# Low parts of 23 weight chunks by an accumulating transfer, one Strassen unit less and a reordered final norm in a residual decoder block

## The chip, the cores and the metric

One core of a Trainium2 chip runs the whole block. Its engines are TensorE (PE; PEld is its weight load), VectorE (DVE), ScalarE (ACT) and GpSimd (POOL); SyncE (SP) issues transfers. The metric is the device time of one execution in microseconds, the median of several runs. The time before is 1468.63 us (three runs, 1467.74 to 1469.05).

## The reference

For 16 learned meta tokens and 256 tokens of 2048 features, in float32:

```python
hn = rms_norm(h, norm_mix_g)
u, gb_in, gc_in, v_in, ga_lin, gbr_lin = split(hn @ w_in)          # 2048 x 12288
y_a = einsum(causal_multiscale_pool(u), pool_w) * pool_scale
y_b = (gb_in * causal_depthwise_conv(gc_in * v_in, conv_w)) @ conv_out_w
h = h + (sigmoid(ga_lin + b) * y_a + sigmoid(gbr_lin + b) * y_b) @ w_o
hn = rms_norm(h, norm_ffn_g)
gate, up = split(hn @ w_gate_up)                                   # 2048 x 11264
h = h + (silu(gate) * up) @ w_down                                 # 5632 x 2048
out = rms_norm(h, norm_final_g)[:, N_META:]
```

## The kernel before

**Split products.** Every float32 weight is split into a high part (the value rounded to the engine's fp32r type) and a low part (the value minus the high part); activations likewise. A product is three matmuls into one accumulation: high by high, high by low, low by high (`mm3`, L500; the second, L503, is the one that reads the weights' low part).

**The weight stream.** All weights come as 528 chunks of 128 partitions x 1024 columns (512 KB), in the order of use. `load` (L109) puts a chunk into one of five raw buffers, by a transfer that SP issues. `split_weights` (L132) makes the high part by a pass of ScalarE (`cut`, L129) and the low part by a subtraction of VectorE that needs the raw chunk and the high part (L130). The parts go into a ring of pairs of tiles, three at first, six from the output projection on (`homes`). `advance` (L164) is called when TensorE takes a job: it gives back the tiles of jobs before that one, issues loads up to five chunks ahead of what is split, and splits as many further jobs as the ring has room for.

**Stages.** After the input projection, pooling, convolution and gates, come 19 groups: two of the output projection, then three rounds of gate/up groups (4, 4 and 3) followed by two down groups each. A group (`group`, L506) has four PSUM banks for its four output blocks ("11", "12", "21", "22": row block and column block of a 256 x 1024 result) and walks a plan of pairs of chunks. A plain pair takes its two chunks one after the other; each gives three matmuls of 512 columns in each of the four banks, 12 in all. A Strassen unit takes a pair as one job of four pairs of tiles, with 7 products of three matmuls, and VectorE builds the sums of blocks for it (L149 to L153). `plan_of` (L714) and `groups` (L720) say at which places units stand. `job_list` (L735) makes the list of jobs from the plans: a plain chunk is a job of kind 1, a unit one of kind 4.

**The end.** In the last down group the last `HELD` = 2 pairs are kept back (`kept`): TensorE first does all others for all banks, then the four kept chunks bank by bank, in the order 11, 12, 21, 22, so that the final norm of a block can start while the next bank is worked on. The last bank is done in two halves of 256 columns. `finish` (L639) takes a finished piece: square with row sums on ScalarE, product with the norm's weights on VectorE, the running sum of squares, and with a row block's last piece the reciprocal root (`rsqrt`, L315), four scalings and the output transfers. Row block 0 ends with bank 12, row block 1 with the second half of 22.

**Order.** Instructions are put into each engine's list when the kernel is built, by priority and by the readiness that is expected then; on the chip each list runs in order, and waits hold it.

Of the kernel before, what the change touches and what calls it, by code (L numbers as in the profile page):

```python
# [10 lines left out]
AF = mybir.ActivationFunctionType  # L11
ALU = mybir.AluOpType
PSUM = bass.MemoryType.PSUM

P = 128
D = 2048
# [21 lines left out]
BC = BW * P  # L38
NC = D // BC
NB = SEQ // P  # L40
FC = FF // BC
# [12 lines left out]
def block_kernel(ctx: ExitStack, tc: tile.TileContext, xT, xn, gfin, consts, spread, weights, out):  # L54
# [6 lines left out]
    nc = tc.nc  # L61
# [44 lines left out]
    raws = {}  # L106
    n_chunks = weights.shape[0]
# [22 lines left out]
        nc.vector.tensor_tensor(out=lo, in0=raw, in1=hi, op=ALU.subtract)  # L130

    def split_weights(j, parts=1):  # L132
        kind, c = jobs[j]
        if kind == 1:
            raw = raws.pop(c)
            hi, lo = part(j)
            step = CH * P // parts
            for s in range(0, CH * P, step):
                q = slice(s, s + step)
                cut(hi[:, q], lo[:, q], raw[:, q])  # L140
            splits[j] = hi, lo
        else:

            r0, r1_ = raws.pop(c), raws.pop(c + 1)
            b12, b11, b22, b21 = r0[:, :BC], r0[:, BC:], r1_[:, :BC], r1_[:, BC:]
            ta = sums.tile([P, 2 * BC], F32, name="ta")
            td = sums.tile([P, 2 * BC], F32, name="td")
            (ah, al), (bh, bl), (ch, cl), (dh, dl) = [part(j) for _ in range(4)]
            nc.vector.tensor_tensor(out=ta[:, :BC], in0=b11, in1=b12, op=ALU.add)  # L149
            cut(bh[:, :BC], bl[:, :BC], b11)  # L150
            nc.vector.tensor_tensor(out=ta[:, BC:], in0=b12, in1=b22, op=ALU.add)
            nc.vector.tensor_tensor(out=td[:, :BC], in0=ta[:, :BC], in1=b22, op=ALU.add)
            nc.vector.tensor_tensor(out=td[:, BC:], in0=td[:, :BC], in1=b21, op=ALU.add)  # L153
            cut(ah, al, ta)
            cut(dh, dl, td)
            cut(ch, cl, r1_)
            splits[j] = {"b11": (bh[:, :BC], bl[:, :BC]),
                         "t1": (ah[:, :BC], al[:, :BC]), "t3": (ah[:, BC:], al[:, BC:]),
                         "t2": (dh[:, :BC], dl[:, :BC]), "t4": (dh[:, BC:], dl[:, BC:]),
                         "b22": (ch[:, :BC], cl[:, :BC]), "b21": (ch[:, BC:], cl[:, BC:])}  # L160
        state["ready"] = j + 1
        state["cut"] = c + (1 if kind == 1 else 2)
# [451 lines left out]
    c = 0  # L614
    tail = {}
    for ci, n in enumerate(CHUNKS):
        af = {"order": iter(["a"] * slots["a"])}
        for i in range(n):
            late = {}
            if c == 0:  # L620
                late[KT // 2 - 4] = lambda: turn_h(NC - 2, "q")
                late[KT // 2 - 2] = lambda: turn_h(NC - 1, "q")
            elif i > 0:
                late[KT // 2 - 3] = lambda c=c, i=i: turn_a(c - 1, af, 2 * (i - 1))
            gate_up(c, late)
            c += 1
        last = ci == len(CHUNKS) - 1
        if last:
            after.close()
            fin = scope.enter_context(tc.tile_pool(name="fin", bufs=1))  # L630
            gf = fin.tile([P, D], F32, name="gf")
            nc.gpsimd.dma_start(out=gf, in_=gfin)
            hg = fin.tile([P, NB, D], F32, name="hg")
            junk = fin.tile([P, BC], F32, name="junk")
            sq = fin.tile([P, NB, NC + 1], F32, name="sq")
            st = fin.tile([P, NB, 7], F32, name="st")
            preload = fin.tile([P, 1], F32, name="preload")

        def finish(b, i, q):  # L639

            h = hn[:, b, q]
            nc.scalar.activation(out=junk[:, : q.stop - q.start], in_=h, func=AF.Square, accum_out=sq[:, b, i : i + 1])
            nc.vector.tensor_tensor(out=hg[:, b, q], in0=h, in1=gf[:, q], op=ALU.mult)
            base, ms, sd, y, y2, m2, r = [st[:, b, i : i + 1] for i in range(7)]
            part_ = sq[:, b, i : i + 1]
            if i == 0:
                nc.scalar.activation(out=preload, in_=ones[:, 0:1], func=AF.Sqrt)
            elif i == 1:
                binary(base, sq[:, b, 0:1], part_, ALU.add)
                mean(base, base)  # L650
            elif i < NC:
                nc.vector.scalar_tensor_tensor(out=base, in0=part_, scalar=1.0 / D, in1=base, op0=ALU.mult, op1=ALU.add)
            else:
                nc.vector.scalar_tensor_tensor(out=ms, in0=part_, scalar=1.0 / D, in1=base, op0=ALU.mult, op1=ALU.add)
                rsqrt(r, ms, sd, y, y2, m2)
                for n_ in (0, 2, 1, 3):
                    o = hg[:, b, n_ * BC : (n_ + 1) * BC]
                    if n_ == 2:
                        nc.scalar.activation(out=o, in_=o, func=AF.Copy, scale=r)
                    else:  # L660
                        nc.vector.tensor_scalar(out=o, in0=o, scalar1=r, scalar2=None, op0=ALU.mult)
                    (nc.sync if n_ < 2 else nc.scalar).dma_start(
                        out=out[b * P : (b + 1) * P, n_ * BC : (n_ + 1) * BC], in_=o)

        for g in range(NC // 2):
            late = {2 * n - 2: lambda: turn_a(c - 1, af, 2 * (n - 1))} if g == 0 else {}
            ends = last and g == NC // 2 - 1
            plain, e, kept, step = group(af, late, HELD if ends else 0)
            keys = [f"{b + 1}{i + 1}" for b in range(NB) for i in range(2)]
            for key in keys:  # L670
                b, cb = int(key[0]) - 1, 2 * g + int(key[1]) - 1
                h = hn[:, b, cb * BC : (cb + 1) * BC]
                binary(h, h, e[key], ALU.add)
            for key in keys:
                b, cb = int(key[0]) - 1, 2 * g + int(key[1]) - 1
                h = hn[:, b, cb * BC : (cb + 1) * BC]
                if ends and key == "22":
                    binary(h, plain[key], h, ALU.add)
                    for i in range(2):
                        q = slice(i * BC // 2, (i + 1) * BC // 2)  # L680
                        p = bank("q")[:, : BC // 2]
                        for n_, (f, k, w) in enumerate(kept):
                            mm3(p, f[f"a2{k + 1}"], [x[:, BC + q.start : BC + q.stop] for x in w], n_ == 0,
                                n_ == len(kept) - 1)
                        binary(h[:, q], p, h[:, q], ALU.add)
                        finish(b, cb + i, slice(cb * BC + q.start, cb * BC + q.stop))
                    continue
                for f, k, w in kept:
                    step(f, k, w, (key,))
                binary(h, plain[key], h, ALU.add)  # L690
                if last:
                    finish(b, NC if cb == NC - 1 else cb, slice(cb * BC, (cb + 1) * BC))
    scope.close()


HELD = 2
STRASSEN = 3
CHUNKS = (4, 4, 3)
FORMS = ("a11", "a12", "a22", "s1", "s2", "s3", "s4", "a21")
# [14 lines left out]
def plan_of(n, at):  # L714

    marked, plain = iter(range(len(at))), iter(range(len(at), n))
    return [(next(marked), True) if i in at else (next(plain), False) for i in range(n)]


def groups():  # L720


    for g in range(NC // 2):
        yield "out", 0, g, plan_of(KT // 2, ((2, 5), (0, 3))[g])
    c = 0
    for n in CHUNKS:
        for i in range(n):
            at = (0, 3) if c + i == 0 else (1, 4) if (n - i) % 2 else (0, 3, 6)
            yield "up", c + i, 0, plan_of(KT // 2, at)
        for g in range(NC // 2):  # L730
            yield "down", c, g, plan_of(2 * n, (0, 3))
        c += n


def job_list(n_chunks):  # L735

    tail = [s for *_, plan in groups() for _, s in plan]
    c = n_chunks - 2 * len(tail)
    jobs = [(1, i) for i in range(c)]
    for s in tail:  # L740
        jobs += [(4, c)] if s else [(1, c), (1, c + 1)]
        c += 2
    return jobs

# [67 lines left out]
```

## Time and profile before

| what | value |
|---|---|
| median of three runs | 1468.63 us (1467.74 to 1469.05) |
| profiled execution | 1469.13 us |
| its span, first to last instruction | 1467.3 us |
| TensorE busy | 1452.2 us, 7682 matmuls |
| VectorE busy | 1137.0 us |
| ScalarE busy | 746.5 us |
| GpSimd busy | 4.9 us |
| mean granted TensorE clock | 0.998 |
| bytes read from HBM | 285.38 MB, 196 GB/s over the span |

A row of the timeline is: start, duration, engine, line, operation, output<-inputs, shape, count, and in brackets the idle time before it with what ended it. Neighbouring rows of the same kind are merged into one with a count. A line can be that of a helper: L243 is `binary`, L129 and L130 are `cut`, L253 and L254 are `split` with a scale.

### The profile page before, as it was taken

How to read it: one execution, taken by the hardware profiler on the slowest of the kernel's cores; microseconds unless marked ns; L12 is line 12 of the kernel's file. 1: busy time of each engine (PE TensorE's matmuls, PEld its weight loads, DVE VectorE, ACT ScalarE, POOL GpSimd, SP SyncE). 2: the span in 40 equal slices, each digit the busy share in tenths (PEclk: the TensorE clock that was granted, in tenths of full speed). 3: DMA queues.
4: the chain of work that ended last, by engine and by line, in shares of the span. 5: the costliest groups of instructions: out<-in, count | busy, mean ns of one | idle time of the engine just before them, and what ended most of it. 6: DMA issues, size and time to landing. Idle time of an engine off the chain costs nothing.

```text
span 1467.3 us, 20054 instructions
## 1 busy us (share of the span) xinstructions
PE 1452.2 (99%) x7682; PEld 1251.5 (85%) x7682; DVE 1137.0 (77%) x1510; ACT 746.5 (51%) x925; POOL 4.9 (0%) x12
## 2 busy tenths in 40 slices
PE   9999999999999999999999999999999999999997
PEld 9999999999888888888888888888888888887886
DVE  7986666666656565658998989988898998788898
ACT  6544444444444444445675556554555555455563
POOL 0000000000000000000000000000000000000000
PEclk9999999999999999999999999999999999999999
DMA  9555555555665656666655557655555765564663
GB/s 334 192 185 186 186 187 187 187 186 182 207 217 190 218 186 214 190 192 217 216 169 190 172 199 219 211 175 197 191 196 188 229 201 185 189 200 159 216 215 115
DMA packets 79984, 288.80 MB, mean 197 GB/s; under 512 B 8976, under 2 KB 9232, under 8 KB 79632
## 3 DMA queue, kind: packets, MB, share of 16 engines
q1 hardware_dynamic: 77760, 279.61, 58.3%
q0 software_dynamic: 1120, 6.29, 1.3%
q10 hardware_dynamic: 1008, 1.61, 0.3%
q8 instruction: 60, 0.98, 0.3%
q14 instruction: 36, 0.29, 0.1%
HBM read 285.38 MB, written 2.10 MB: 196 GB/s over the span
## 4 chain that ended last, share of the span: by engine, by line
PE 96%; DVE 2%; DMA 1%; ACT 0%; issue 0%; ACTq 0%; DVEq 0%
PE acc L504 17%; PE acc L502 17%; PE acc L503 17%; PE acc L200 6%; PE acc L199 6%; PE acc L198 6%; PE acc L219 6%; PE acc L220 6%; PE acc L221 6%; PE acc L213 4%; PE acc L214 2%; PE acc L277 1%; DVE lo L130 1%; DMA raw<-weights 1%; DVE act L243 0%; PE acc L367 0%
## 5 line engine op out<-in xcount | busy, mean ns | idle before, releaser
L130 DVE TENSOR_TENSOR lo<-raw,hi 128x1024 fp32r<-128x1024 f32 (+1 forms) x529 | 618.3, 1177 | 241.9 <-ACT hi L129 238.9
L129 ACT CAST hi<-raw 128x1024 fp32r<-128x1024 f32 (+1 forms) x529 | 533.0, 1016 | 528.2 <-PE acc L504 154.5
L502 PE MATMUL acc<-hi,hp 128*128 128x512 f32 x678 | 263.3, 391 | 2.5 <-ACT hp L253 1.0
L503 PE MATMUL acc<-lo,hp 128*128 128x512 f32 x678 | 263.6, 389 | 0.0
L504 PE MATMUL acc<-hi,hp 128*128 128x512 f32 x678 | 263.6, 390 | 0.0
L219 PE MATMUL acc<-xp,hi 128*128 128x258 f32 (+3 forms) x704 | 198.7, 282 | 0.0
L220 PE MATMUL acc<-xp,hi 128*128 128x258 f32 (+3 forms) x704 | 198.5, 282 | 0.0
L221 PE MATMUL acc<-xp,lo 128*128 128x258 f32 (+3 forms) x704 | 198.4, 282 | 0.0
L503 PE MATMUL acc<-lo,act 128*128 128x512 f32 (+1 forms) x468 | 181.3, 387 | 0.0
L502 PE MATMUL acc<-hi,act 128*128 128x512 f32 (+1 forms) x468 | 180.7, 388 | 0.3 <-DVE act L243 0.3
L504 PE MATMUL acc<-hi,act 128*128 128x512 f32 (+1 forms) x468 | 180.2, 388 | 0.3 <-DVE act L251 0.3
L502 PEld LDWEIGHTS acc<-hi,hp 128*128 128x128 f32 x678 | 127.0, 188 | 30.8 <-ACT hi L129 2.5
L503 PEld LDWEIGHTS acc<-lo,hp 128*128 128x128 f32 x678 | 127.3, 188 | 26.4
L504 PEld LDWEIGHTS acc<-hi,hp 128*128 128x128 f32 x678 | 127.3, 188 | 26.3
L219 PEld LDWEIGHTS acc<-xp,hi 128*128 128x128 f32 x704 | 132.4, 188 | 0.7
L221 PEld LDWEIGHTS acc<-xp,lo 128*128 128x128 f32 x704 | 132.5, 188 | 0.0
L220 PEld LDWEIGHTS acc<-xp,hi 128*128 128x128 f32 x704 | 132.4, 188 | 0.0
L502 PEld LDWEIGHTS acc<-hi,act 128*128 128x128 f32 x468 | 87.8, 188 | 18.8 <-ACT act L250 0.8
L504 PEld LDWEIGHTS acc<-hi,act 128*128 128x128 f32 x468 | 87.7, 188 | 18.9 <-DVE act L251 1.2
L503 PEld LDWEIGHTS acc<-lo,act 128*128 128x128 f32 x468 | 87.9, 188 | 17.9
L198 PE MATMUL acc<-hi,xp 128*128 128x512 f32 x256 | 100.0, 390 | 0.0
L200 PE MATMUL acc<-hi,xp 128*128 128x512 f32 x256 | 99.6, 389 | 0.0
(133 smaller groups left out, 1747.0 us busy)
## 6 DMA issues: line engine op xcount, KB each, us to landing
raw<-weights SPq DMA_DIRECT2D x527, 512.0 KB, 3.8
sp<-spread POOLq DMA_DIRECT2D x4, 768.0 KB, 5.9
hn<-xn POOLq DMA_DIRECT2D x1, 2048.0 KB, 11.9
xall<-xT SPq DMA_DIRECT2D x7, 272.0 KB, 7.2
gf<-gfin POOLq DMA_DIRECT2D x1, 1024.0 KB, 6.8
out<-hg ACTq DMA_DIRECT2D x4, 256.0 KB, 3.4
out<-hg SPq DMA_DIRECT2D x4, 256.0 KB, 3.1
raw<-weights ACTq DMA_DIRECT2D x2, 256.0 KB, 4.9
```

The lines of the kernel that those rows point to most:

```text
L129: nc.scalar.copy(out=hi, in_=raw)
L130: nc.vector.tensor_tensor(out=lo, in0=raw, in1=hi, op=ALU.subtract)
L198: nc.tensor.matmul(out=p, lhsT=a[:, 0, t], rhs=hi, start=first, stop=False)
L199: nc.tensor.matmul(out=p, lhsT=a[:, 0, t], rhs=lo, start=False, stop=False)
L200: nc.tensor.matmul(out=p, lhsT=a[:, 1, t], rhs=hi, start=False, stop=last)
L213: nc.tensor.matmul(out=p, lhsT=hi, rhs=a[:, :, off : off + SEQ], start=first, stop=False)
L219: nc.tensor.matmul(out=p, lhsT=hi, rhs=a[:, 0, off : off + n], start=first, stop=False)
L220: nc.tensor.matmul(out=p, lhsT=hi, rhs=a[:, 1, off : off + n], start=False, stop=False)
L221: nc.tensor.matmul(out=p, lhsT=lo, rhs=a[:, 0, off : off + n], start=False, stop=last)
L502: nc.tensor.matmul(out=p, lhsT=ah, rhs=wh, start=first, stop=False)
L503: nc.tensor.matmul(out=p, lhsT=ah, rhs=wl, start=False, stop=False)
L504: nc.tensor.matmul(out=p, lhsT=al, rhs=wh, start=False, stop=last)
```

## The change

In the job list each job gets a third entry, `added`. It is true for a plain chunk of the output projection or later, if the job before it isn't one and the last five jobs are all plain; with the kernel's plans that holds for 23 chunks. For these `split_weights` makes the high part as before, then ScalarE writes the negated high part into the low tile, and GpSimd issues a transfer of the same chunk from HBM with an addition into that tile: low = -high + weight. VectorE's subtraction isn't issued.

In the last group of the last round the plan has one Strassen unit (at place 0) instead of two (at 0 and 3), and `HELD` is 3: six plain chunks are kept. They are the last six jobs, and the second, fourth and sixth of them are added ones.

`finish` is cut into `square`, `weigh`, `gather` and `finish`. For the last bank both halves are done first (matmuls, addition, square), then the first half is weighed, both sums are gathered, and the second half is weighed between them and the reciprocal root.

```diff
+            raw = raws.pop(c)
+            hi, lo = part(j)
+            nc.scalar.copy(out=hi, in_=raw)
+            nc.scalar.activation(out=lo, in_=hi, func=AF.Copy, scale=-1.0)
+            nc.gpsimd.dma_start(out=lo, in_=weights[c], accum_op=ALU.add)
+            splits[j] = hi, lo
...
-        def finish(b, i, q):
...
+        def square(b, i, q):
+            nc.scalar.activation(out=junk[:, : q.stop - q.start], in_=hn[:, b, q], func=AF.Square,
+                                 accum_out=sq[:, b, i : i + 1])
...
+        def weigh(b, q):
+            nc.vector.tensor_tensor(out=hg[:, b, q], in0=hn[:, b, q], in1=gf[:, q], op=ALU.mult)
+        def gather(b, i):
...
+        def finish(b, between=lambda: None):
+            ms, sd, y, y2, m2, r = [st[:, b, i : i + 1] for i in range(1, 7)]
+            between()
+            rsqrt(r, ms, sd, y, y2, m2)
...
-                        finish(b, cb + i, slice(cb * BC + q.start, cb * BC + q.stop))
+                        square(b, cb + i, where[i])
+                    weigh(b, where[0])
+                    gather(b, cb)
+                    gather(b, cb + 1)
+                    finish(b, lambda: weigh(b, where[1]))
...
-HELD = 2
+HELD = 3
...
-            yield "down", c, g, plan_of(2 * n, (0, 3))
+            yield "down", c, g, plan_of(2 * n, (0,) if c + n == FC and g == 1 else (0, 3))
...
-        jobs += [(4, c)] if s else [(1, c), (1, c + 1)]
+        for k in range(1 if s else 2):
+            added = not s and len(jobs) > n_chunks - 2 * len(tail) + 5 and not jobs[-1][2] \
+                and all(j[0] == 1 for j in jobs[-5:])
+            jobs.append((4 if s else 1, c + k, added))
```

## Rows read from the trace of the kernel before

**Rows 1.** The page: busy us by engine, and the chain that ended last.
```profile
PE 1452.2 (99%) x7682; PEld 1251.5 (85%) x7682; DVE 1137.0 (77%) x1510; ACT 746.5 (51%) x925; POOL 4.9 (0%) x12
...
PE 96%; DVE 2%; DMA 1%; ACT 0%; issue 0%; ACTq 0%; DVEq 0%
```
**Rows 2.** Waits of TensorE: waiting line, waited for, us in total, times, longest.
```profile
PE acc L502 <- ACT hp L253: 1.0, 1, 1.0
PE acc L502 <- ACT hi L129: 1.0, 2, 0.5
PE acc L502 <- DVE act L243: 0.8, 2, 0.5
```
**Rows 3.** Windows, the last group: length, busy us by engine, clock, DMA share, GB/s.
```profile
1425.70:1457.40 31.70, 31.61 (x151) 26.48 (x149) 30.97 (x54) 16.24 (x29) 0.00 (x0) 1.00 0.24 84
```
**Rows 4.** Timeline of TensorE, kept steps: eight matmuls apart, then 23 halves apart.
```profile
1446.12 0.39 PE L502 MATMUL acc<-hi,act 128*128 128x512 f32 x1
...
1447.93 0.39 PE L504 MATMUL acc<-hi,act 128*128 128x512 f32 x1
...
1454.28 0.28 PE L502 MATMUL acc<-hi,act 128*128 128x256 f32 x1
...
1457.03 0.28 PE L504 MATMUL acc<-hi,act 128*128 128x256 f32 x1
```
**Rows 5.** Groups by form: busy us, mean ns, idle before and what ended it.
```profile
L130 DVE TENSOR_TENSOR lo<-raw,hi 128x1024 fp32r<-128x1024 f32 x485 | 588.7, 1222 | 239.7 <-ACT hi L129 236.9
L129 ACT CAST hi<-raw 128x1024 fp32r<-128x1024 f32 x485 | 506.2, 1052 | 494.7 <-PE acc L200 145.7 <-PE acc L504 123.1 <-PE acc L220 108.4
```
**Rows 6.** DMA issues of the page: KB each, median us from issue to landing.
```profile
raw<-weights SPq DMA_DIRECT2D x527, 512.0 KB, 3.8
sp<-spread POOLq DMA_DIRECT2D x4, 768.0 KB, 5.9
hn<-xn POOLq DMA_DIRECT2D x1, 2048.0 KB, 11.9
...
gf<-gfin POOLq DMA_DIRECT2D x1, 1024.0 KB, 6.8
```
**Rows 7.** Timeline, one chunk: ScalarE's high part, TensorE's first use of the low part.
```profile
985.12 1.05 ACT L129 CAST hi<-raw 128x1024 fp32r<-128x1024 f32 x1
...
998.47 0.39 PE L503 MATMUL acc<-lo,act 128*128 128x512 f32 x1
```
**Rows 8.** Timeline of ScalarE and TensorE at the start of unit m = 4, first gate/up group.
```profile
768.21 1.05 ACT L129 CAST hi<-raw 128x1024 fp32r<-128x1024 f32 x1 [0.48 <-PE acc L277]
769.16 0.47 ACT L253 ACTIVATE hp<-acc,cst 128x256 fp32r<-128x256 f32 x1
...
769.68 0.50 PE L502 MATMUL acc<-hi,hp 128*128 128x512 f32 x1 [1.05 <-ACT hp L253]
```
**Rows 9.** Timeline of TensorE, end of the first kept bank, with two L502 merged.
```profile
1448.16 0.62 PE L502 MATMUL acc<-hi,act 128*128 128x512 f32 x2
1448.61 0.39 PE L503 MATMUL acc<-lo,act 128*128 128x512 f32 x1
```
**Rows 10.** Timeline of ScalarE and VectorE, a unit's addition in front of a split.
```profile
778.22 1.05 ACT L129 CAST hi<-raw 128x1024 fp32r<-128x1024 f32 x1 [1.30 <-issue]
...
780.32 0.69 DVE L151 TENSOR_TENSOR ta<-raw 128x512 f32<-128x512 f32 x1 [1.51 <-DMA raw<-weights]
780.92 1.22 DVE L130 TENSOR_TENSOR lo<-raw,hi 128x1024 fp32r<-128x1024 f32 x1
```
**Rows 11.** Timeline behind the last matmul.
```profile
1457.35 0.42 DVE L243 TENSOR_TENSOR hn<-acc,hn 128x256 f32<-128x256 f32 x1 [0.31 <-PE acc L504]
...
1457.69 1.27 DVE L661 TENSOR_SCALAR hg<-hg,st 128x512 f32<-128x512 f32 x3
...
1459.80 0.20 ACT L316 ACTIVATE st<-st 128x1 f32<-128x1 f32 x1 [1.21 <-DVE st L654]
...
1460.82 1.28 DVE L661 TENSOR_SCALAR hg<-hg,st 128x512 f32<-128x512 f32 x3
```

More of the change, by code (lines that the diff above doesn't have):

```diff
@@ L132, in split_weights @@
     def split_weights(j, parts=1):
-        kind, c = jobs[j]
-        if kind == 1:
+        kind, c, added = jobs[j]
+        if added:
+            raw = raws.pop(c)
[4 more added lines that the diff above has]
+            splits[j] = hi, lo
+        elif kind == 1:
             raw = raws.pop(c)
@@ L637, in block_kernel @@
             preload = fin.tile([P, 1], F32, name="preload")
-        def finish(b, i, q):
[L641 to L645, printed above, removed]
+        def square(b, i, q):
+            nc.scalar.activation(out=junk[:, : q.stop - q.start], in_=hn[:, b, q], func=AF.Square,
+                                 accum_out=sq[:, b, i : i + 1])
@@ L646, in finish @@
             if i == 0:
                 nc.scalar.activation(out=preload, in_=ones[:, 0:1], func=AF.Sqrt)
-            elif i == 1:
+        def weigh(b, q):
+            nc.vector.tensor_tensor(out=hg[:, b, q], in0=hn[:, b, q], in1=gf[:, q], op=ALU.mult)
+        def gather(b, i):
+            base, ms, part_ = st[:, b, 0:1], st[:, b, 1:2], sq[:, b, i : i + 1]
+            if i == 1:
                 binary(base, sq[:, b, 0:1], part_, ALU.add)
                 mean(base, base)
[L651 to L663, printed above, removed]
@@ new lines, in gather @@
+            elif i > 1:
+                nc.vector.scalar_tensor_tensor(out=base if i < NC else ms, in0=part_, scalar=1.0 / D, in1=base,
+                                               op0=ALU.mult, op1=ALU.add)
+        def finish(b, between=lambda: None):
+            ms, sd, y, y2, m2, r = [st[:, b, i : i + 1] for i in range(1, 7)]
+            between()
+            rsqrt(r, ms, sd, y, y2, m2)
+            for n_ in (0, 2, 1, 3):
+                o = hg[:, b, n_ * BC : (n_ + 1) * BC]
+                if n_ == 2:
+                    nc.scalar.activation(out=o, in_=o, func=AF.Copy, scale=r)
+                else:
+                    nc.vector.tensor_scalar(out=o, in0=o, scalar1=r, scalar2=None, op0=ALU.mult)
+                (nc.sync if n_ < 2 else nc.scalar).dma_start(
+                    out=out[b * P : (b + 1) * P, n_ * BC : (n_ + 1) * BC], in_=o)
@@ L678, in block_kernel @@
                     binary(h, plain[key], h, ALU.add)
-                    for i in range(2):
-                        q = slice(i * BC // 2, (i + 1) * BC // 2)
+                    lots = [slice(i * BC // 2, (i + 1) * BC // 2) for i in range(2)]
+                    where = [slice(cb * BC + q.start, cb * BC + q.stop) for q in lots]
+                    for i, q in enumerate(lots):
                         p = bank("q")[:, : BC // 2]
@@ L691, in block_kernel @@
                 if last:
-                    finish(b, NC if cb == NC - 1 else cb, slice(cb * BC, (cb + 1) * BC))
+                    i, q = NC if cb == NC - 1 else cb, slice(cb * BC, (cb + 1) * BC)
+                    square(b, i, q)
+                    weigh(b, q)
+                    gather(b, i)
+                    if i == NC:
+                        finish(b)
     scope.close()
-HELD = 2
+HELD = 3
 STRASSEN = 3
@@ L738, in job_list @@
     c = n_chunks - 2 * len(tail)
-    jobs = [(1, i) for i in range(c)]
+    jobs = [(1, i, False) for i in range(c)]
     for s in tail:
-        jobs += [(4, c)] if s else [(1, c), (1, c + 1)]
+        for k in range(1 if s else 2):
+            added = not s and len(jobs) > n_chunks - 2 * len(tail) + 5 and not jobs[-1][2] \
+                and all(j[0] == 1 for j in jobs[-5:])
+            jobs.append((4 if s else 1, c + k, added))
         c += 2
```

## The prediction

> **What bounds the kernel now.** I read the page's busy line first, then its chain that ended last, then TensorE's own waits, then single stretches of the timeline. The reader should see that TensorE is busy for 1452.2 of 1467.3 us, that 96% of the chain is TensorE, and that VectorE (1137.0 us) and ScalarE (746.5 us) have idle time to spare [rows 1]. The three largest waits of TensorE for the two of them inside the stages come to 1.0 + 1.0 + 0.8 = 2.8 us [rows 2]. So work taken from VectorE or ScalarE can give back 2.8 us at most, and a change pays only where it shortens TensorE's own list of matmuls, one of these waits, or the tail behind the last matmul. In the last group TensorE is busy for 31.61 of 31.70 us at a granted clock of 1.00, with VectorE at 30.97 us beside it [rows 3].
>
> The profiled execution took 1469.13 us: a span of 1467.3 and 1.8 around it. The median of the runs is 1468.63, half a microsecond less. I make the sum as a difference and add it to the median. A measurement of this kernel can tell about 0.2%, 2.9 us, from no change.
>
> **Part 1: matmuls of the last group.** One Strassen unit (7 products of 3 matmuls, 21) becomes two plain chunks (12 matmuls each). Before, the group has 21 + 4 x 12 + 21 = 90 matmuls of 512 columns, then 4 kept chunks for three banks (36), then 24 of 256 columns for the last bank. After, it has 21 + 4 x 12 = 69, then 6 kept chunks for three banks (54), and 36 of 256 columns. Eight steps of the 512-column list take 1447.93 - 1446.12 = 1.81 us, 0.226 each; 23 steps of the 256-column list take 1457.03 - 1454.28 = 2.75 us, 0.120 each [rows 4]. The sum is 12 x 0.120 - 3 x 0.226 = **+0.76 us**, all on the path. Against that VectorE loses one unit's four additions and its split in a stretch where it had been full; TensorE did not wait there [rows 3], so I give nothing for it.
>
> **Part 2: the 23 chunks.** For each, VectorE's subtraction goes (1222 ns), ScalarE gets a second pass over 128x1024, for which I take the time of its first, 1052 ns [rows 5], and GpSimd issues a transfer that reads the weights once more and adds them to the negated high part. VectorE gains 23 x 1.22 = 28 us and ScalarE pays 23 x 1.05 = 24 us; both are off the path except as below. Raw buffers come free earlier, after ScalarE's first pass instead of VectorE's subtraction. GpSimd is otherwise empty; its load of the final norm's weights waits for the end of the last gate/up group, and the accumulating transfers queued behind it belong to the last group and can't start earlier anyway. So that queue costs nothing.
>
> No row shows an accumulating transfer. From below I bound it by the plain 512 KB load at 3.8 us. GpSimd's own plain loads take 5.9 us for 768 KB and 11.9 for 2048 KB; the line between gives 4.7 for 512 KB. From above I take the 1024 KB load, 6.8 us, because the destination has to be read as well as the source [rows 6]. I take 4.7, on the same queue, and keep 3.8 and 6.8. The Trainium skill, "Collectives: The Full Stack", section "The bandwidth ceiling: the fold count and why AG ≠ RS ≠ AR", says that an add in a DMA engine is slow not for the addition but because it takes two source reads, which halves its pace. By that page of the Trainium skill the upper bound would be the likelier value, and the sum 3.3 us larger if nothing fills in; no run here shows it yet.
>
> Is this latency covered? The ring has six pairs of tiles, and a plain chunk holds TensorE for 12 x 0.226 = 2.7 us, so a pair that comes free is needed again five chunks, 13.6 us, later. For the tightest of the first 20 chunks, the high part is done at 985.12 + 1.05 = 986.17 and TensorE first reads the low part at 998.47 [rows 7]: 12.3 us, the loosest has 14.9. After ScalarE's second pass some 11.2 us are left, against 3.8 to 6.8. So 20 of the 23 cost nothing on this account; the cover goes only beyond 11.2 us, and the transfer would then cost its excess at up to 20 places.
>
> ScalarE's second pass also delays what is queued behind it. I looked behind each of the 20. Nearly everywhere forms for a later stage or idle time follows. One place touches TensorE: at 768.21 ScalarE makes a high part, only then at 769.16 the form that TensorE has waited 1.05 us for [rows 8]. If the second pass is put between, that wait grows by 0.95 us. The form stands earlier in the program than the chunk's split, so the scheduler has a reason to prefer it; I take 0 and keep **0 to +0.95**.
>
> **Part 3: the last chunk.** This is where the cover is gone. The last three added chunks are among the six kept ones, which TensorE first uses for one bank only, 3 x 0.226 = 0.68 us each. The last one's tiles come free when the last unkept chunk is done. TensorE then has five kept chunks (3.4 us) and one matmul, 3.6 us, before it reads that low part. The chain to it is two passes of ScalarE, 2.1 us, and the transfer: 5.9, 6.8 or 8.9 us. In the program's order TensorE would wait 2.3, 3.2 or 5.3 us. (The one two chunks before gets its tiles 5.4 us earlier and is needed 1.4 earlier: 4.1 us more room, in time except at the upper bound, and its wait would be part of the same.) But the order on an engine is fixed when the kernel is built, by readiness as then expected: in this same stretch two L502 follow each other at 1448.16, before the L503 whose low part was late [rows 9]. Matmuls of the next bank can fill in, for as long as the transfer was expected to take. The trace shows such expectations for loads to be short: VectorE stood 1.51 us at L151 for a load, while the split behind it had its high part ready at 778.22 + 1.05 = 779.27 [rows 10]. I take **+2.0 us** for the wait that is left, by that 1.51 and the 3.2 of the program's order, and keep 0 to 5.3.
>
> **Part 4: the final norm.** Behind the last matmul VectorE now adds (1457.35), but then does three scalings of the first row block (1457.69, 1.27 us), two weighings and the sums, so that the square root starts at 1459.80 and the last scalings at 1460.82 [rows 11]. After, the first row block ends one longer bank earlier (18 matmuls of 512 columns and 36 of 256 run behind it, 8.4 us), and its scalings lie beside TensorE. Behind the addition, done at 1457.77, come the half's square with its read-out (0.6), two hand-overs (0.2) and one sum (0.15): the root at about 1458.75, a gain of **-1.05 us**. One weighing of 0.42 may still stand in the way, or a little more be won: -0.6 to -1.3. The output transfers behind it stay the same.
>
> The sum is 0.76 + 0 + 2.0 - 1.05 = +1.7 us: 1468.63 + 1.7 = **1470.3**.
>
> **The rivals.**
> - The order foresees the last transfer. Nothing waits: 0.76 - 1.05 = -0.3, 1468.3. For it speaks [rows 9], against it [rows 10].
> - The accumulating transfer is as slow as its upper bound or slower. The wait is 5.3 us or more and the form of 769 us may be late too: 0.76 + 5.3 + 0 to 0.95 - 1.05 = +5.0 to +6.0, 1473.6 to 1474.6. This is the one that ends slower: with 2.0 replaced by the wait, 0.2% is passed from a wait of 3.2 us, that is from a transfer of 4.7 us with nothing filled in, and beyond 11.2 us the other 20 chunks join in. For it speaks that no load of GpSimd's over 512 KB takes less than 5.9 us [rows 6]; against it, that the load queue is empty at that point. The rule cited above from the Trainium skill leads to this rival.
> - VectorE's relief ends TensorE's waits: -2.8, without a wait at the end 1468.3 - 2.8 = 1465.5, faster by just over 0.2%. Against it: the two waits for a high part lie where the eleventh gate/up group follows the tenth, and the tenth has no added chunk; the longest, at 769 us, is for ScalarE, which gets more to do [rows 8].
> - The 23 transfers change nothing, because the subtractions that they remove lay in VectorE's idle time (1467.3 - 1137.0 = 330 us in all). Then parts 1 and 4 alone are left, 1468.3 again: the time can't tell it from the first rival, VectorE's busy time can.
>
> **How the numbers follow.** My forecast has 0.50, no wait at the end 0.20 (with the last rival), the slow transfer 0.17, the relief 0.13. Of the forecast's half, about a tenth lies above +2.9. So faster 0.13, same 0.65, slower 0.22. The range leaves a tenth on each side: 1466.2, between the relief and the first rival, to 1474.0, in the middle of the slow transfer.
>
> **What would show it.** The waits of TensorE should have one new line, for a DMA into the low part, near the start of the kept steps, of 1.5 to 3 us; the 20 others none. The issue list should show 23 transfers from GpSimd with 4 to 7 us to landing. The square root of the second row block should start some 1.7 us after the last matmul's start instead of 2.8. The last group's list should be 0.76 us longer without its wait. I am wrong if transfers take over 11 us, if waits appear at many added chunks, or if the waits of [rows 2] are gone.

## The result and the profile after

The changed kernel takes 1476.22 us (median of six runs, 1475.41 to 1478.12), against 1468.3 for the kernel before on the same chip. The ratio is 1.0052, with an interval of 1.0041 to 1.0062: slower by half a per cent. The forecast was 1470.3, and the range ended at 1474.0.

The profiled execution took 1476.38 us with a span of 1474.3, so the span grew by 7.0 us over that of before. The page of the changed kernel, busy time by engine and the chain that ended last:

```profile
PE 1454.7 (99%) x7691; PEld 1252.5 (85%) x7691; DVE 1109.8 (75%) x1481; ACT 767.5 (52%) x946; POOL 24.9 (2%) x35
...
PE 90%; DVE 5%; DMA 2%; ACT 1%; issue 1%; ACTq 0%; POOL 0%; DVEq 0%; POOLq 0%
```

Against [rows 1] VectorE does 27.2 us less and ScalarE 21.0 us more: the work moved as the change says. The chain is TensorE for 90% instead of 96%. That share alone doesn't show a loss: the run no_added below has 91% at nearly the time of before. What shows it is the list of TensorE's waits (line, waited for, us in total, times, longest), with the first line of VectorE's waits for loads:

```profile
PE acc L511 <- DMA lo<-weights: 4.2, 3, 2.1
PE acc L512 <- DVE act L259: 1.7, 2, 1.4
PE acc L510 <- ACT hp L261: 1.2, 1, 1.2
...
DVE ta L157 <- DMA raw<-weights: 38.1, 24, 5.0
```

L510 to L512 are now the three matmuls of a product, L157 is a unit's first addition, L259 the split of an activation, L261 that of a form, and L138 to L140 make the low part of an added chunk. Two things are new beside [rows 2]. TensorE waits for three low parts. And VectorE waits 38.1 us for raw loads instead of 18.6, which comes out at TensorE as a wait of 1.4 us for an activation.

Set against the trace of before, TensorE's matmuls stand 0.4 us later by 1208 us, 2.1 later by 1262, 2.3 later at 1418, and 8.2 later at the last matmul (its start went from 1457.03 to 1465.19). Behind that the tail is 1.2 us shorter. So 2.3 us were lost before the last group, 5.9 in it, and 1.2 won behind it: 7.0.

**The last three low parts.** The page's issue list of the changed kernel (KB each, median us from issue to landing):

```profile
raw<-weights SPq DMA_DIRECT2D x527, 512.0 KB, 4.1
lo<-weights POOLq DMA_DIRECT2D x23, 512.0 KB, 8.8
```

The added transfer takes 8.8 us in the median, the slowest of the 23 takes 10.1. Its three last issues, ScalarE's work ahead of them, and the matmuls that waited for them (timeline of the changed kernel: start, duration, and in brackets the idle time before it with what ended it):

```profile
1434.54 1.03 ACT L138 CAST hi<-raw 128x1024 fp32r<-128x1024 f32 x1
1435.47 0.63 ACT L649 ACTIVATE junk<-hn 128x512 f32<-128x512 f32 x1
...
1436.10 1.05 ACT L139 ACTIVATE lo<-hi 128x1024 fp32r<-128x1024 f32 x1
...
1446.54 1.05 ACT L138 CAST hi<-raw 128x1024 fp32r<-128x1024 f32 x1 [3.02 <-DMA raw<-weights]
...
1437.44 0.86 POOL L140 DMA_DIRECT2D lo<-weights  x1 [41.98 <-ACT lo L139]
1442.86 0.85 POOL L140 DMA_DIRECT2D lo<-weights  x1 [4.56 <-DVE lo L130]
1448.97 0.86 POOL L140 DMA_DIRECT2D lo<-weights  x1 [5.26 <-ACT lo L139]
...
1445.56 0.50 PE L511 MATMUL acc<-lo,act 128*128 128x512 f32 x1 [0.84 <-DMA lo<-weights]
...
1446.83 0.61 PE L510 MATMUL acc<-hi,act 128*128 128x512 f32 x2
1449.59 0.50 PE L511 MATMUL acc<-lo,act 128*128 128x512 f32 x1 [2.15 <-DMA lo<-weights]
...
1454.53 0.50 PE L511 MATMUL acc<-lo,act 128*128 128x512 f32 x1 [1.24 <-DMA lo<-weights]
```

From issue to first use it is 8.1, 6.7 and 5.6 us: 1437.44 to 1445.56, 1442.86 to 1449.59, 1448.97 to 1454.53. Each transfer ends in a wait of its own, and in front of each wait at most one matmul of the next product was put first (the merged L510 at 1446.83). The first transfer was late because a square of the previous result (L649) lay between ScalarE's two passes over the chunk, the last because its raw load came late (3.02 us). That load is the last of the stream. It was issued at 1439.4 us here and in no_added below; its time to landing is this here, with the first added transfer under way, and then in no_added:

```profile
DMA to landing us min/median/max: 7.1/7.1/7.1
```

```profile
DMA to landing us min/median/max: 4.1/4.1/4.1
```

So the waits of the last group also hold some of what the transfers do to the raw loads. The idle time of TensorE at the three low parts is 0.84 + 2.15 + 1.24 = 4.2 us. From start to start the three steps are 1.0, 2.3 and 1.4 us longer than 0.227, and the matmul behind each takes 0.11 more: 5.0 us.

**The wait at 1210 us** (timeline of the changed kernel):

```profile
1200.43 0.86 POOL L140 DMA_DIRECT2D lo<-weights  x1 [36.37 <-PE acc L512]
...
1205.50 0.69 DVE L157 TENSOR_TENSOR ta<-raw 128x512 f32<-128x512 f32 x1 [2.71 <-DMA raw<-weights]
...
1211.46 0.42 DVE L259 TENSOR_TENSOR act<-acc,act 128x256 fp32r<-128x256 f32 x1
1211.93 0.50 PE L512 MATMUL acc<-hi,act 128*128 128x512 f32 x1 [1.43 <-DVE act L259]
```

The same sum in the kernel before:

```profile
1203.14 0.69 DVE L149 TENSOR_TENSOR ta<-raw 128x512 f32<-128x512 f32 x1 [0.25 <-DMA raw<-weights]
```

With an added transfer under way, a raw load comes 2.71 us too late for a unit's sum; before it was 0.25 there. VectorE's list is full from 1205.50 on, so the split of the activation behind the sums comes late, and TensorE stands 1.43 us.

**The last group and the tail** (windows of the changed kernel, the last group as in [rows 3]: length, busy us by engine, clock, DMA share, GB/s):

```profile
1427.70:1465.60 37.90, 33.55 (x161) 27.32 (x160) 26.86 (x50) 18.59 (x31) 2.57 (x3) 1.00 0.53 141
```

TensorE is idle for 4.35 of 37.90 us, at full granted clock, where [rows 3] had 0.09 of 31.70. The timeline of the changed kernel around the last matmul:

```profile
1459.87 1.28 DVE L675 TENSOR_SCALAR hg<-hg,st 128x512 f32<-128x512 f32 x3
...
1465.19 0.28 PE L512 MATMUL acc<-hi,act 128*128 128x256 f32 x1
...
1466.77 0.20 ACT L324 ACTIVATE st<-st 128x1 f32<-128x1 f32 x1 [0.23 <-DVE st L663]
```

The second square root starts 1.58 us after the last matmul's start; in [rows 4, 11] it was 2.77. The first row block's three scalings, which stood in its way there, now lie beside TensorE at 1459.87.

### The profile page after: what moved, and what is told of

Its sections match the earlier page's. It is cut to its first block, busy times and chain, and to the rows that moved or that the text cites. A ratio compares the mean times of both kernels' runs of the same rounds, so it can differ in the third digit from the quotient of the medians.

```text
span 1474.3 us, 20132 instructions
## 1 busy us (share of the span) xinstructions
PE 1454.7 (99%) x7691; PEld 1252.5 (85%) x7691; DVE 1109.8 (75%) x1481; ACT 767.5 (52%) x946; POOL 24.9 (2%) x35
## 4 chain that ended last, share of the span: by engine, by line
PE 90%; DVE 5%; DMA 2%; ACT 1%; issue 1%; ACTq 0%; POOL 0%; DVEq 0%; POOLq 0%
PE acc L512 15%; PE acc L511 15%; PE acc L510 15%; PE acc L208 6%; PE acc L207 6%; PE acc L206 6%; PE acc L228 6%; PE acc L227 6%; PE acc L229 6%; PE acc L221 4%; PE acc L222 2%; DVE lo L130 2%; DMA raw<-weights 2%; PE acc L285 1%; DVE act L251 1%
## 5 line engine op out<-in xcount | busy, mean ns | idle before, releaser
L130 DVE TENSOR_TENSOR lo<-raw,hi 128x1024 fp32r<-128x1024 f32 (+1 forms) x506 | 592.1, 1177 | 244.9 <-ACT hi L129 242.4
L129 ACT CAST hi<-raw 128x1024 fp32r<-128x1024 f32 (+1 forms) x506 | 510.4, 1015 | 498.1 <-PE acc L208 145.7
L510 PE MATMUL acc<-hi,hp 128*128 128x512 f32 x678 | 263.3, 391 | 2.6 <-ACT hp L261 1.2
L512 PE MATMUL acc<-hi,hp 128*128 128x512 f32 x678 | 263.7, 390 | 0.0
L512 PE MATMUL acc<-hi,act 128*128 128x512 f32 (+1 forms) x471 | 181.4, 387 | 1.8 <-DVE act L259 1.7
L510 PE MATMUL acc<-hi,act 128*128 128x512 f32 (+1 forms) x471 | 181.6, 388 | 0.6 <-DVE act L251 0.5
L510 PEld LDWEIGHTS acc<-hi,hp 128*128 128x128 f32 x678 | 127.0, 188 | 31.0 <-ACT hi L129 2.5
L512 PEld LDWEIGHTS acc<-hi,hp 128*128 128x128 f32 x678 | 127.3, 188 | 26.4
L512 PEld LDWEIGHTS acc<-hi,act 128*128 128x128 f32 x471 | 88.4, 188 | 20.8 <-DVE act L259 3.1
L510 PEld LDWEIGHTS acc<-hi,act 128*128 128x128 f32 x471 | 88.4, 188 | 19.1 <-ACT act L258 1.0
```

Of the source, the lines that this page charges most:

```text
L129: nc.scalar.copy(out=hi, in_=raw)
L510: nc.tensor.matmul(out=p, lhsT=ah, rhs=wh, start=first, stop=False)
L512: nc.tensor.matmul(out=p, lhsT=al, rhs=wh, start=False, stop=last)
```

## The experiments

Each ratio is to the kernel before on the same chip; that kernel's own median was 1468.1 to 1468.3 us there.

The theory after this reading: the plan and the norm cost nothing on balance; the other 20 covered chunks cost some 2.5 us through the raw loads and nothing through their own low parts; the last three cost 4 to 5. Rivals: the plan or the norm is the loss; ScalarE's second pass is; the plain transfer, not its addition, is.

### Plan and norm without added chunks: no_added

```diff
-            added = not s and len(jobs) > n_chunks - 2 * len(tail) + 5 and not jobs[-1][2] \
-                and all(j[0] == 1 for j in jobs[-5:])
+            added = False
```

> The changed kernel with no chunk marked as added: only the shorter plan, the six kept chunks and the reordered norm are left. If the 23 transfers cost all that was lost (theory), the last group costs 0.76 us more in matmuls and the tail 1.05 to 1.2 less, without a new wait of TensorE: 1468.3 + 0.76 - 1.1 = 1468.0. If the keeping of six chunks itself makes TensorE wait (rival), waits stay in the last group and the time lies at 1470 to 1473.

Measured: 1468.9 us, ratio 1.0003 (0.9993 to 1.0013). VectorE's wait for raw loads is back to that of before (waits of no_added; L159 is a unit's second addition):

```profile
DVE ta L157 <- DMA raw<-weights: 18.1, 18, 1.9
...
DVE ta L159 <- DMA raw<-weights: 2.0, 3, 1.5
```

One small wait is new. Timeline of TensorE in no_added, in the kept steps:

```profile
1446.00 0.50 PE L511 MATMUL acc<-lo,act 128*128 128x512 f32 x1 [0.24 <-DVE lo L130]
```

From its first unit to its last matmul the last group is 1.30 us longer than before: the 0.76 of matmuls, and this wait for a low part that VectorE makes, 0.41 at the first step and 0.11 at the next. The shorter tail pays that back. So the whole loss lies with the 23 chunks, and no_added is the base for the others. Against it the changed kernel's matmuls fall back by 1.5 us at 1210, 1.2 at 1415 and 4.5 in the kept steps.

### Added chunks except the last three: last_off; only the last three: last_only

```diff
-    return jobs
+    return [(k, i, a and i < 510) for k, i, a in jobs]      # last_off
+    return [(k, i, a and i >= 510) for k, i, a in jobs]     # last_only
```

> The 20 transfers ahead of the last group stay, the three in it go back to VectorE. Theory: the three waits of the last group, 5.0 us with their restarts, go, the wait near 1210 us (1.7) and the small ones at 769 and 954 us stay: 1476.2 - 5.0 = 1471.2. Rival, that the last group's waits come from late raw loads or ScalarE's queue: waits of 2 us or more stay there and the time is 1473 or more.

> The other half: the 20 go back to VectorE, the three of the last group stay. Theory: the waits at 769, 954 and 1210 us are those of the kernel before, the last group's 5.0 us stay: 1476.2 - 2.2 = 1474.0. Rival, that the 20 transfers cost nothing by themselves and the wait near 1210 us is a chance of the built order: 1476.

Measured: last_off 1471.46, ratio 1.0023 (1.0014 to 1.0033); last_only 1472.86, ratio 1.0033 (1.0021 to 1.0045). Over no_added that is +2.6 and +4.0, together 6.6 where all 23 cost 7.3; last_only came out 1.1 under its expectation. Waits of last_off, then its timeline:

```profile
DVE ta L157 <- DMA raw<-weights: 39.9, 24, 4.5
```

```profile
1393.44 0.69 DVE L157 TENSOR_TENSOR ta<-raw 128x512 f32<-128x512 f32 x1 [2.27 <-DMA raw<-weights]
...
1416.19 0.70 PE L510 MATMUL acc<-hi,act 128*128 128x512 f32 x2 [0.65 <-DVE act L251]
```

No wait for a transferred low part is left in last_off (one of 0.3 us for VectorE's is, as in no_added), so the cover of the 20 held; what is left is VectorE's wait for raw loads and TensorE's behind it. Between the two rows VectorE's list has 1.0 us of idle time, so the delay stays. The place shifts from run to run: the wait at 1210 was 0.2 us here, and 0.4 fell at 954 and 1.3 at 1415. All three lie in the first down group of a round, where TensorE turns the activations of the last gate/up group (`turn_a`) and waits for VectorE's work on them, which stands in VectorE's list behind a unit's sum. Of last_only the waits, one row of TensorE's timeline, and windows:

```profile
PE acc L511 <- DMA lo<-weights: 4.0, 2, 2.8
```

```profile
1447.43 0.50 PE L511 MATMUL acc<-lo,act 128*128 128x512 f32 x1 [2.76 <-DMA lo<-weights]
```

```profile
1440.00:1448.00 8.00, 4.00 (x17) 2.66 (x16) 3.96 (x6) 2.72 (x3) 1.32 (x2) 1.00 0.77 177
1448.00:1452.00 4.00, 4.00 (x12) 3.13 (x11) 0.00 (x0) 0.00 (x0) 0.00 (x0) 0.57 0.66 115
```

Two waits here instead of three, 4.0 us against 4.2. This is the slowest of the six runs, 1474.0 against their median of 1472.86. The low clock of the second window is taken up in the last section.

### A plain transfer in place of the added one: plain_pool

```diff
-            nc.gpsimd.dma_start(out=lo, in_=weights[c], accum_op=ALU.add)
+            nc.gpsimd.dma_start(out=lo, in_=weights[c])
```

> All 23 transfers stay on GpSimd's queue, but without the addition, so that the low tile gets the whole weight; the remainder that it should hold is left out. If the addition makes the transfer slow (theory: the destination is read as well), landing falls from 8.8 us to some 4.7, the waits of the last group shrink by 3 to 4 us and the wait near 1210 us goes: about 1471. If GpSimd's queue or the sharing with the raw loads is the cause (rival), landing stays above 7 us and the time near 1475.

Measured: 1471.61, ratio 1.0023 (1.0013 to 1.0032). Here the low tile gets the weights themselves and no remainder is formed. Of plain_pool the issue list, the waits, and one issue in the timeline:

```profile
lo<-weights POOLq DMA_DIRECT2D x23, 512.0 KB, 6.8
```

```profile
PE acc L511 <- DMA lo<-weights: 1.4, 2, 0.9
DVE ta L157 <- DMA raw<-weights: 27.0, 23, 3.2
```

```profile
1440.79 0.53 POOL L140 DMA_DIRECT2D lo<-weights  x1 [4.65 <-ACT lo L139]
```

A plain transfer on that queue lands after 6.8 us, not the 4.7 of my line; the time came out as expected, the landing didn't. The last of the 23, issued when the raw loads had all landed, has this in plain_pool:

```profile
DMA to landing us min/median/max: 3.6/3.6/3.6
```

With the addition the last one landed after 5.5 us. Judging by these two transfers, what runs beside them costs either kind some 3 us, and the addition some 2. In the median the addition makes it 8.8, and is worth 1476.2 - 1471.6 = 4.6 us of time; the transfer without it 2.7 over no_added.

### ScalarE's second pass alone: pass_only

```diff
+            cut(hi, lo, raw)
+            spare = sink.tile([P, CH * P], F32R, name="spare")
+            nc.scalar.activation(out=spare, in_=hi, func=AF.Copy, scale=-1.0)
-            nc.scalar.copy(out=hi, in_=raw)
-            nc.scalar.activation(out=lo, in_=hi, func=AF.Copy, scale=-1.0)
-            nc.gpsimd.dma_start(out=lo, in_=weights[c], accum_op=ALU.add)
```

> As the run with the spare tile, but without the transfers: ScalarE's second pass alone. Theory: nothing hangs on it, 1468.9, as without added chunks, with VectorE's waits for raw loads near 18 us. Rival, that the second pass in ScalarE's queue delays forms and high parts: 1471.

Measured: 1468.44, ratio 1.0003 (0.9994 to 1.0013); VectorE's wait for raw loads 18.5 us. The pass is free, and so it isn't the loss.

### The transfers alone: traffic, traffic20

traffic is pass_only with the added transfer into the spare tile behind the pass. traffic20 has no pass: at the 20 first places GpSimd copies one column of the new high part into a spare tile that ScalarE fills once, and issues the added transfer into it, while VectorE subtracts as before.

```diff
             cut(hi, lo, raw)
...
+            nc.gpsimd.tensor_copy(out=spare[:, 0:1], in_=hi[:, 0:1])
+            nc.gpsimd.dma_start(out=spare, in_=weights[c], accum_op=ALU.add)
...
+    return [(k, i, a and i < 510) for k, i, a in jobs]
```

> VectorE's subtraction is back in all 23 chunks; ScalarE's second pass and GpSimd's accumulating transfer run at the same places, but into a spare tile that nobody reads (one small tile is moved to another pool to make room). Theory, the transfers hold up the raw loads on the shared engines: VectorE's waits for raw loads at the units' first sum stay near 38 us against 18 without transfers, TensorE has no wait for a low part, and the time stays 2 to 3 us over the kernel without added chunks, 1471 to 1472. Rival, that only TensorE's waits for low parts cost anything: 1468.9.

> VectorE's subtraction is back everywhere. Ahead of the last group, at the 20 places, GpSimd copies one column of the high part into a spare tile and then issues the accumulating transfer into it; ScalarE has no second pass and no engine but GpSimd waits for the spare tile, which the run with the waiting ScalarE could not say of itself. So only the traffic is added. Theory, the transfers hold up the raw loads: VectorE's waits for raw loads at a unit's first sum rise from 18 to 30 us or more, and the time is that of the kernel with the 20 transfers in use, 2 to 3 us over the one without, 1471 to 1472. Rival, that the use of the transfers costs and not their traffic: 1468.9.

Measured: traffic 1489.54, ratio 1.0146 (1.0130 to 1.0161). It tells little: ScalarE's waits have 33.6 us for its own spare tile, which is a cost of the experiment.

traffic20: 1475.73, ratio 1.0054 (1.0040 to 1.0067), 6.8 us over no_added, far more than expected. Waits of traffic20:

```profile
DVE ta L161 <- DMA raw<-weights: 33.3, 23, 3.6
DVE ta L163 <- DMA raw<-weights: 11.6, 9, 2.1
...
PE acc L515 <- ACT hi L129: 3.5, 4, 1.3
PE acc L517 <- DVE act L263: 1.7, 3, 0.7
```

(L161 and L163 are the first two unit sums here, L515 to L517 the product's matmuls.) Twenty transfers that nobody on TensorE's path reads delay the raw loads: VectorE's two waits for them are 44.9 us instead of 20.1 in no_added, and TensorE waits for high parts and activations. By the matmuls' offsets against no_added it loses 2.1 us at 954, 2.4 at 1210 and 0.6 at 1415, the same three places as in last_off, and 0.7 near 750. The spare tile itself held ScalarE for 0.4 us in all. That the two kinds of load hinder each other is shown by this; whether on the DMA engines or at the memory it doesn't tell.

### Half the columns by transfer: half

```diff
-            nc.scalar.activation(out=lo, in_=hi, func=AF.Copy, scale=-1.0)
-            nc.gpsimd.dma_start(out=lo, in_=weights[c], accum_op=ALU.add)
+            nc.scalar.activation(out=lo[:, :BC], in_=hi[:, :BC], func=AF.Copy, scale=-1.0)
+            nc.gpsimd.dma_start(out=lo[:, :BC], in_=weights[c, :, :BC], accum_op=ALU.add)
+            nc.vector.tensor_tensor(out=lo[:, BC:], in0=raw[:, BC:], in1=hi[:, BC:], op=ALU.subtract)
```

> All 23 chunks, but the transfer adds only the first 512 columns of the low part (256 KB); VectorE subtracts the other 512. If landing goes by bytes, it falls from 8.8 to 4.5 to 5.5 us, TensorE's waits in the last group from 5.0 to about 1 us, and the raw loads are held up half as much: 1470 to 1471. If a fixed part dominates (rival), landing stays above 7 us and the time at 1474 or more.

Measured: 1478.95, ratio 1.0080 (1.0065 to 1.0096): not faster than the whole. The time is the rival's, the landing of 6.3 us lies between the two. The four runs go from 1477.24 us at a mean granted clock of 0.998, the profiled one, to 1482.05 at 0.994, so part of the median is clock. Of half the issue list and the longest of TensorE's waits (L512 reads the weights' low part):

```profile
lo<-weights POOLq DMA_DIRECT2D x23, 256.0 KB, 6.3
```

```profile
PE acc L512 <- DMA lo<-weights: 3.4, 1, 3.4
```

Half the bytes saves 2.5 of 8.8 us. Two sizes make a line with a fixed part of 8.8 - 2 x 2.5 = 3.8 us (worked out from these two medians alone). The idle time at low parts hardly shrinks, 3.4 us against 4.2. By the matmuls' offsets against no_added, half loses 5.0 us before the last group and 3.1 in it, where the changed kernel loses 2.6 and 4.5. VectorE has half its work on these chunks back, but its waits for raw loads at a unit's first sum are 23.6 us, fewer than the changed kernel's 38.1; why half loses more before the last group isn't shown.

### The relief alone: relief20

The 20 first places get the second pass, but neither a transfer nor a subtraction; the low tile holds the negated high part and no remainder is formed.

```diff
-            nc.gpsimd.dma_start(out=lo, in_=weights[c], accum_op=ALU.add)
...
+    return [(k, i, a and i < 510) for k, i, a in jobs]
```

> Ahead of the last group the 20 added chunks have ScalarE's second pass and neither VectorE's subtraction nor a transfer; their low part stays the negated high part, so the remainder that it should hold is left out. This is the relief without the traffic: with the runs without added chunks (1468.9), with traffic alone (1475.7) and with both (1471.5) it closes a square. Theory, the relief is worth something only where raw loads are late: TensorE's waits inside the stages fall at most from 2.9 to 1 us and the time lies at 1467 to 1468.5. Rival, that the 4.2 us between traffic alone and both are owed to the relief everywhere: 1464.5 to 1465.5.

Measured: 1470.34, ratio 1.0014 (1.0005 to 1.0023), runs from 1468.25 to 1472.01: over the expected 1467 to 1468.5. VectorE's freed time is worth nothing, as the forecast had it. The 1.4 us over no_added are not explained: the profiled execution took 1468.54, among the fastest of the eleven, so its trace doesn't hold what the median lost. This stays open. Of its waits:

```profile
DVE ta L156 <- DMA raw<-weights: 24.0, 22, 2.1
```

(L156 is a unit's first addition here.) With less to do, VectorE stands 24.0 us for raw loads without any transfer, against 18.1 in no_added. So some 6 of the 38.1 us of the changed kernel may be VectorE being there earlier; traffic20, where VectorE's work is whole, tells better what the transfers do.

The four cases for the 20 places are then: neither transfer nor relief 1468.9, transfer alone 1475.7, relief alone 1470.3, both 1471.5. The relief has a value only as a repair: it gives back 4.2 of the 6.8 us that the transfers cost. With the subtraction goes also the raw buffer's wait for it; which of the two repairs isn't separated.

### The tail's two causes: norm_only, held_only

norm_only is the kernel before with the reordered norm; held_only is no_added with the old norm (`finish` as in the kernel before).

```diff
-                        finish(b, cb + i, slice(cb * BC + q.start, cb * BC + q.stop))
+                        square(b, cb + i, where[i])
+                    weigh(b, where[0])
+                    gather(b, cb)
+                    gather(b, cb + 1)
+                    finish(b, lambda: weigh(b, where[1]))
```

> The kernel before with the reordered norm alone: plan, two kept pairs and low parts as before. If the gain behind the last matmul comes from the order of the weighings and sums, it is there whole: 1468.3 - 1.1 = 1467.2. If it comes from the first row block ending a longer bank earlier, half of it or less is left: 1467.8 to 1468.3.

> The shorter plan and six kept chunks with the norm in its old order, no added chunks. 0.76 us more matmuls; if the tail's gain comes from the earlier end of the first row block, most of it is there: 1468.3 + 0.76 - 0.8 = 1468.3. If it comes from the order of the norm: 1469.0 or more.

Measured: norm_only 1467.97, ratio 0.9997 (0.9988 to 1.0006); held_only 1468.31, ratio 0.9999 (0.9991 to 1.0008). Timelines from the last matmul to the square root, norm_only and then held_only:

```profile
1455.52 0.28 PE L512 MATMUL acc<-hi,act 128*128 128x256 f32 x1
1456.18 1.27 DVE L675 TENSOR_SCALAR hg<-hg,st 128x512 f32<-128x512 f32 x3
1458.29 0.20 ACT L324 ACTIVATE st<-st 128x1 f32<-128x1 f32 x1 [1.22 <-DVE st L663]
```

```profile
1456.85 0.28 PE L512 MATMUL acc<-hi,act 128*128 128x256 f32 x1
1458.42 0.20 ACT L324 ACTIVATE st<-st 128x1 f32<-128x1 f32 x1 [0.23 <-DVE st L662]
```

From matmul to root it is 2.77 us in norm_only, as before, and 1.57 in held_only, as after. So the tail's gain comes from the shorter plan with its six kept chunks alone; the reordering changes nothing, since the first row block's scalings still stand in VectorE's list ahead of the second one's sums.

### The first row block's scalings on GpSimd: pool_scale

```diff
-                    nc.vector.tensor_scalar(out=o, in0=o, scalar1=r, scalar2=None, op0=ALU.mult)
+                    (nc.vector if b else nc.gpsimd).tensor_scalar(out=o, in0=o, scalar1=r, scalar2=None, op0=ALU.mult)
```

> The kernel before with the reordered norm, and the three scalings of the first row block that VectorE did behind the last matmul given to GpSimd. In the run with the reordered norm alone they stand 1.27 us in VectorE's list ahead of the last sums, so that nothing was won there. Theory, those scalings are what the tail waits for: the square root starts about 1.1 us earlier, 1468.0 - 1.1 = 1466.9, which would beat both kernels. Rival, that GpSimd's slower scalings or its output transfers end last: 1468 or more.

Measured, for norm_only with this edit: 1470.65, ratio 1.0016 (1.0007 to 1.0025). Timeline of GpSimd and of the second square root:

```profile
1456.37 4.66 POOL L675 TENSOR_SCALAR hg<-hg,st 128x512 f32<-128x512 f32 x3 [62.79 <-DVE st L328]
...
1461.46 0.20 ACT L324 ACTIVATE st<-st 128x1 f32<-128x1 f32 x1 [3.64 <-POOL hg L675]
```

Three scalings take 4.66 us there against 1.27 on VectorE, and the square root comes 5.2 us behind the last matmul's start, against 2.77 in norm_only: ScalarE waits 3.64 us for GpSimd, since an output transfer of a block that GpSimd scales stands in its list ahead of the root. The rival was right. No kernel of these beats the kernel before by more than the measurement can tell.

## Why the prediction was wrong

- **What bounds it** held: relief of VectorE is worth nothing to TensorE (relief20, and the rival "relief" with it), and nothing but TensorE's list, its waits and the tail, and in last_only the clock, is seen to have moved the time. The ceiling of 2.8 us left out three shorter waits of TensorE for the same two engines in the trace of before, 0.6, 0.3 and 0.2 us; with them it is 3.9.
- **Part 1** held for the matmuls, +0.76. The plan also brings a wait of 0.5 us for VectorE's low part (no_added, and held_only too), which I had excluded by [rows 3]; in the changed kernel the transfers' waits stand in its place.
- **Part 2, the transfer's length**, is the first step that failed: 4.7 taken, 6.8 as the upper bound, 8.8 measured. Beside the weight stream a plain transfer of this size on that queue already takes 6.8 (plain_pool), and the addition puts 2.0 on top; why the two loads of 768 and 2048 KB gave too low a line isn't shown. The argument that the load queue is empty at that point held for the last transfer alone, which landed after 5.5. The Trainium skill ("Collectives: The Full Stack", "The bandwidth ceiling: the fold count and why AG ≠ RS ≠ AR") says of a collective's reduce step that an add halves the pace for its second read. This points the right way, but the landing grew by 8.8 / 6.8 = 1.29 only. It led to the rival that came closest.
- **Part 2, the cover of the 20**, held for the low parts themselves: 8.8, and 10.1 for the slowest, are under the 11.2 us of room, and there was no wait for a low part before the kept steps. The form at 769 us was waited for 1.2 us (the line L261 of the waits above) instead of 1.0: inside 0 to +0.95, but no_added, without second passes, has 1.3 there, so they added nothing.
- **Part 2, "that queue costs nothing"**, is the second step that failed, and the term that was missing. I looked for what is queued behind the transfers on GpSimd and not for what they do to SP's loads. 23 more transfers of 512 KB lie in the way of the raw loads; these come late at VectorE's unit sums, which had little room, and TensorE stands in the first down group of each round: +2.6 us (last_off against no_added), 6.8 without VectorE's relief (traffic20).
- **Part 3** is the third: +2.0 taken, 5.0 measured. I let one wait stand for all three ("its wait would be part of the same"), which holds only if the chunks behind are waiting anyway; in the trace each transfer was issued after ScalarE's own late pass, and each ended in a new wait; the last raw load, slowed from 4.1 to 7.1 us by the first transfer, made the last one late. Matmuls put first by the order filled at most one step each, as [rows 10] had warned. [rows 9], which spoke for more, shows only the order: no idle time stands before its L503, so that low part was not late on the chip.
- **Part 4** held in size, -1.2 against -1.05, and in its reason: one bank more behind the first row block. held_only and norm_only separate it from the reordering, to which I gave nothing of its own.
- **The sum** with the measured terms is 0.76 + 2.3 + 5.0 - 1.2 = 6.9 us against a span that grew by 7.0. The slow transfer's rival, 1473.6 to 1474.6, had the transfer's price in its direction but not the raw loads' 2.3 to 2.6; with them it would have been 1475.9 to 1477.2. That this meets the 1476.2 is partly luck: its 5.3 us were one wait at one chunk, and the measured 5.0 are three, the longest of 2.15.
- **The signs of being wrong** that the prediction names did not come up: no transfer took over 11 us, no waits stood at many added chunks, and the waits of [rows 2] were not gone. What gave it away was the issue list, 8.8 us where 4 to 7 were forecast.

## What to carry to other kernels

A transfer that takes work off an idle engine is paid for on the DMA side: before it is called free, find the other stream's nearest consumer with no room, here VectorE's unit sums, and ask what a load that comes 2 us later does there. The price of a transfer on a queue is read from one of its size that ran beside the same traffic, and a chain of producer, pass and transfer that ends in the last kept chunks is summed for each chunk by itself. When a tail shortens, undo each edit alone: here the shorter plan with its six kept chunks did it all and the reordered norm nothing.

## What the runs showed of the hardware

- An accumulating 512 KB transfer issued by GpSimd beside the weight stream lands after 8.8 us in the median, a plain one after 6.8; 256 KB with addition after 6.3. With the raw loads at an end the last of each landed after 5.5 and 3.6 us (512 KB with addition, plain). The issue itself holds GpSimd 0.86 us with the addition, 0.53 without.
- Two streams of loads hinder each other: 20 added transfers raised VectorE's waits for raw loads from 20.1 to 44.9 us (traffic20), and the last raw load took 7.1 us beside the first kept chunk's transfer instead of 4.1.
- In last_only, after two waits of 1.24 and 2.76 us within 6 us, TensorE's granted clock fell to the level of 1.2 GHz: the window from 1448 to 1452 has 0.57 in the mean, and eight steps from 1448.23 to 1451.63 took 3.40 us, 0.43 each instead of 0.227, a loss of 1.6 us; before that, from 1440 to 1448 and still at 1.00, TensorE had been busy for 4.0 us and idle for as long. In the changed kernel's own profile, with waits of 0.84, 2.15 and 1.24, the clock stayed at 1.00. So such waits can cost more than their length.
- Three scalings of 128x512 by a column take 4.66 us on GpSimd (pool_scale) and 1.27 on VectorE (norm_only).
